# Token-major projections with 512 moving weight columns and one PSUM bank per token tile

## The chip, the core and the metric

The kernel runs on one core of one Trainium2 chip. The metric is the device time of one execution in microseconds. A core has TensorE (PE in the profile, with its weight loads shown as PEld), VectorE (DVE), ScalarE (ACT), GpSimd (POOL) and SyncE (SP), which here issues most DMAs.

## The reference

The reference is a two-layer diffusion backbone over 256 latent tokens and 256 context tokens of width 1024. Each layer normalizes and modulates its input and multiplies it by one combined input projection; three token mixers then work on slices of the result, are merged through gates and an output projection, and are followed by a mixture of experts. Cut to the lines that matter here:

```python
pl = split_cols(h @ w_in)            # latent tokens; pc = the same of the context tokens
qa = apply_rope(rms_norm(to_heads(pl[0], A_HEADS, HEAD_DIM), g_qk[0]), cos, sin)
ka = apply_rope(rms_norm(to_heads(pl[1], A_KV_HEADS, HEAD_DIM), g_qk[1]), cos, sin)
ya, ya_c = gqa_branch(qa, ka, va, qa_c, ka_c, va_c, need_ctx)
qb = rms_norm(to_heads(pl[3], NA_HEADS, HEAD_DIM), g_qk[2])
kb = rms_norm(to_heads(pl[4], NA_HEADS, HEAD_DIM), g_qk[3])
vb = to_heads(pl[5], NA_HEADS, HEAD_DIM)
yb, yb_c = na_branch(qb, kb, vb, qb_c, kb_c, vb_c, rpb, rows, need_ctx)
ym, ym_c = mlstm_branch(...)
y, yc = merge((ya, yb, ym), pl[11], n_tok), ...
x = x + gt1 * y
x = x + gt2 * hier_moe(h, ...)
```

In the second (last) layer the context tokens need no output, so queries are computed for the 256 latent tokens alone, and keys and values for all 512.

## The kernel before

**Tiling.** The normalized input is held feature-major as eight slabs of 128 features by 512 tokens, each split into a high and a low part (`hh`, `hl`) whose sum is the full value. Weights are split in the same way by `wsplit` (lines 207 to 225): ScalarE writes the rounded high part (line 221), VectorE the rest (line 222), in pieces of 128 x 1024 for which there are three buffers each (`whi`, `wlo`). A product is three matmuls into the same PSUM region (`mm3`, lines 332 to 335): high by high, high by low, low by high.

**Token-major and feature-major projections.** `proj_t` (line 490) holds 128 x 128 blocks of the input stationary, one block per token tile of 128 tokens, and moves weight columns: the result has tokens on partitions. One call covers a chunk of 256 weight columns, so that two token tiles share one PSUM bank of 512 columns, and four token tiles take two banks. `proj_f` (line 510) does the opposite: weights stand, 512 tokens (256 in layer 1 where only latent tokens are wanted) move.

**The eight chunks.** After the projections of mixer C (the mLSTM), lines 877 to 901 compute in order: one chunk with the key and value of mixer A (`win[0]`), two chunks of its query, two of the key of mixer B, two of its value and two of its query. Two chunks make one pair of 512 columns. Value chunks are copied to SBUF by VectorE (line 895). Query and key chunks go through `qk_chunk` (line 576), bank by bank: a square on ScalarE (526), a sum over each head on VectorE (528), an addition (532 or 534), a power of -0.5 on GpSimd (536), and a multiplication on VectorE (540), which is the last reader of the bank; latent query tiles of mixer A are then rotated by `do_rope` (VectorE and GpSimd, lines 553 to 558). The transposes back to feature-major (`to_T`, line 561: four 128 x 128 transposes into one bank, lines 570 to 574 evict it on ScalarE) are put into a list `later` and written into the program after the matmuls of the next chunk.

**Fillers.** After its matmuls `proj_t` calls `mod_fill(1)`, which computes one of the adaLN modulation chunks that later stages need: a 1 MB load, 16 matmuls of 32 stationary columns (line 238), an eviction, two transposes (243).

**PSUM.** Of the eight banks four are in the pool `mm`, which serves all projections, the transposes of `to_T` and the modulation chunks; two (`at`), one (`tr`) and one (`ao`) serve the mLSTM scans and the attentions.

**Order of the work.** The scans of the mLSTM stand ahead of the eight chunks in the source, the attention of mixer A behind them. The program is built with `schedule_with_timeline_sim=True` (line 1530): each engine's order of instructions is fixed when the program is built, by a model of the timeline, and parts that stand apart in the source are interleaved. At run time each engine takes its instructions in that order.

Of the kernel before, what the change touches and what calls it, by code (L numbers as in the profile page):

```python
# [24 lines left out]
KT = D // 128  # L25
# [20 lines left out]
def tile_backbone(ctx: ExitStack, tc: tile.TileContext, T, out):  # L46
    nc = tc.nc
# [26 lines left out]
    def t2(shape, dtype=F32, tag="t2", bufs=4):  # L74
        return tp.tile([128] + list(shape), dtype, tag=tag, name=nm(tag), bufs=bufs)
# [4 lines left out]
    def pmm():  # L80
        return bank("mm", 4)
# [53 lines left out]
    ident = cst("ident", [128])  # L135
# [220 lines left out]
    def mixers(l, need_ctx, xsrc, stats):  # L356
# [133 lines left out]
        def proj_t(src, ntt, wid=256):  # L490
# [16 lines left out]
            flush()  # L507
            return banks, views

# [12 lines left out]
        def qknorm(pv, H, is_q):  # L522

            sq = t2([512])
            sqv = sq[:, :2 * H * 64].rearrange("p (t h d) -> p t h d", t=2, d=64)
            nc.scalar.activation(sqv, pv, AF.Square)
            st = small([2 * H])
            nc.vector.tensor_reduce(
                st.rearrange("p (t h) -> p t h", t=2), sqv, axis=AX.X, op=ALU.add)
            v = small([2 * H])  # L530
# [4 lines left out]
            r = small([2 * H])  # L535
            nc.gpsimd.tensor_tensor(out=r, in0=v, in1=powm[:, :2 * H], op=ALU.pow)  # L536
            o = t2([512])
            ov = o[:, :2 * H * 64].rearrange("p (t h d) -> p t h d", t=2, d=64)
            rb = r.rearrange("p (t h) -> p t h", t=2).unsqueeze(3).to_broadcast([128, 2, H, 64])
            nc.vector.tensor_tensor(out=ov, in0=pv, in1=rb, op=ALU.mult)  # L540
            return ov

        def do_rope(x, H, a):
            o = t2([512])
            ov = o[:, :2 * H * 64].rearrange("p (t h d) -> p t h d", t=2, d=64)
            tm = t2([512])
            tv = tm[:, :2 * H * 64].rearrange("p (t h d) -> p t h d", t=2, d=64)

            def tb(j):
                return ropet[:, :, a, j, :].unsqueeze(2).to_broadcast([128, 2, H, 32])  # L550
# [10 lines left out]
        def to_T(parts, H, dst, gain, lat_gain):  # L561

            for p in range(H // 2):
                q = pmm()
                for t in range(2 * len(parts)):
                    src = parts[t // 2][:, t % 2, 2 * p:2 * p + 2, :].rearrange("p h d -> p (h d)")
                    nc.tensor.transpose(q[:, 128 * t:128 * t + 128], src, ident)
                n = 256 * len(parts)
                if lat_gain:
                    nc.scalar.activation(dst(p)[:, :n], q[:, :n], AF.Copy, scale=gain)  # L570
                else:
                    nc.scalar.copy(dst(p)[:, :256], q[:, :256])
                    if n > 256:
                        nc.scalar.activation(dst(p)[:, 256:], q[:, 256:n], AF.Copy, scale=gain)

        def qk_chunk(banks, H, cols, a, is_q, dst, rope_lat):
            parts = []
            for b, bk in enumerate(banks):
                pv = bk.rearrange("p (t c) -> p t c", t=2)[:, :, cols].rearrange("p t (h d) -> p t h d", d=64)
                x = qknorm(pv, H, is_q)  # L580
                if b == 0 and rope_lat:
                    x = do_rope(x, H, a)
                parts.append(x)
            later.append(lambda: to_T(parts, H, dst, gqkT[:, l, a:a + 1], not rope_lat))

        later = []

        def flush():
            while later:
                later.pop(0)()  # L590
# [290 lines left out]
        qk_chunk(banks, 2, slice(0, 128), 1, False, lambda p: kTA, True)  # L881
# [6 lines left out]
        for c in range(2):  # L888
            banks, views = proj_t(win[3 + c], 4)
            qk_chunk(banks, 4, slice(0, 256), 3, False, lambda p, c=c: kTB[:, 2 * c + p], False)  # L890
        vB = s8("qkv", [4, 512])
        for c in range(2):
            banks, views = proj_t(win[5 + c], 4)
            for b in range(2):
                nc.vector.tensor_copy(
                    vB[:, 2 * b:2 * b + 2, 256 * c:256 * c + 256], banks[b].rearrange("p (t c) -> p t c", t=2))
        qTB = s8("qkv", [4, N])
        for c in range(2):
            banks, views = proj_t(win[7 + c], ntq)
            qk_chunk(banks, 4, slice(0, 256), 2, True, lambda p, c=c: qTB[:, 2 * c + p], False)  # L900
        flush()
# [533 lines left out]
def _pack(inputs):  # L1435
    a = {k: np.asarray(v) for k, v in inputs.items()}
    P = 128

    def kmaj(w):
# [30 lines left out]
        w[:, :, cols].reshape(DEPTH, KT, P, 28, 256).transpose(0, 3, 2, 1, 4))  # L1470
    pc = np.concatenate([np.arange(3328, 3328 + 256), np.arange(4352, 4368)])
# [63 lines left out]
```

## Time and profile before

| | |
|---|---|
| median of three runs | 1634.6 us (1631.34 to 1635.05) |
| profiled execution | 1629.37 us |
| its span, first to last instruction | 1627.5 us |
| mean granted TensorE clock | 0.972 of full speed |
| busy: TensorE, VectorE, ScalarE, GpSimd | 1529.6, 788.3, 571.8, 183.2 us |

In a row of a timeline the first number is the start in microseconds from the start of the span, the second the duration; then come engine, source line, operation, what is written and read, partitions x elements, the number of merged instructions and, in brackets, idle time of the engine before it and what ended it. A matmul's duration holds its passage through the array, and successive ones overlap: the spacing of starts tells what one costs in a stream.

### The profile page before, as it was taken

The page shows a single profiled execution, that of the slowest core. Times are in us where ns is not written, and L with a number is a line of the kernel's source. Part 1 is how long each engine was busy: PE and PEld are TensorE (multiplying, and loading weights), DVE is VectorE, ACT ScalarE, POOL GpSimd, SP SyncE. Part 2 cuts the span into 40 slices and gives each one's busy share as a digit, 9 for nine tenths or more (in the row PEclk, how much of TensorE's full clock was granted, in tenths as well). Part 3 has the DMA queues.
Part 4 walks back from the last instruction along what each step waited for, and adds up shares of the span by engine and source line. Part 5 has one row for each costly group of instructions (what it writes and reads, how often), then busy time and mean ns, then how long its engine had stood idle before and what let it go on. Part 6 is the DMA issues. An engine that isn't in the chain of part 4 may idle for free. (4 is left out here: it accounts for less than half of the span.)

```text
span 1627.5 us, 26096 instructions
## 1 busy us (share of the span) xinstructions
PE 1529.6 (94%) x10725; PEld 1058.8 (65%) x10725; DVE 788.3 (48%) x1774; ACT 571.8 (35%) x1125; POOL 183.2 (11%) x162
## 2 busy tenths in 40 slices
PE   5999999999999999989999997999999999897875
PEld 3688789767767778844434435989978789632221
DVE  4637943443345425363333457378456556441222
ACT  4425642443344333131211135356355444211100
POOL 2200320100011003010000003003101112100000
PEclk9999999999999999989999998999999999898888
DMA  8552334323322154349999994542225448699998
GB/s 303 194 172 79 108 107 156 117 76 115 127 98 84 40 179 149 121 166 382 375 398 413 377 409 185 209 142 74 91 104 175 169 148 325 231 411 416 417 418 325
DMA packets 57199, 349.26 MB, mean 215 GB/s; under 512 B 6912, under 2 KB 8032, under 8 KB 20336
## 3 DMA queue, kind: packets, MB, share of 16 engines
q1 hardware_dynamic: 54720, 341.02, 54.9%
q10 hardware_dynamic: 1616, 5.24, 0.9%
q0 software_dynamic: 736, 1.24, 0.4%
q8 instruction: 88, 1.44, 0.4%
q14 instruction: 39, 0.32, 0.1%
HBM read 344.33 MB, written 3.15 MB: 213 GB/s over the span
## 5 line engine op out<-in xcount | busy, mean ns | idle before, releaser
L222 DVE TENSOR_TENSOR wlo<-wraw,whi 128x1024 fp32r<-128x1024 f32 (+1 forms) x152 | 190.6, 1254 | 169.3 <-ACT whi L221 154.2
L333 PE MATMUL mm<-h,whi 128*128 128x512 f32 (+1 forms) x656 | 226.9, 348 | 0.0
L334 PE MATMUL mm<-h,whi 128*128 128x512 f32 (+1 forms) x656 | 223.4, 342 | 0.0
L335 PE MATMUL mm<-h,wlo 128*128 128x512 f32 (+1 forms) x656 | 222.2, 342 | 0.0
L221 ACT CAST whi<-wraw 128x1024 fp32r<-128x1024 f32 (+1 forms) x152 | 155.6, 1026 | 172.3 <-PE mm L334 68.7
L333 PE MATMUL mm<-whi,h 128*128 128x256 f32 (+1 forms) x640 | 183.1, 289 | 0.0
L335 PE MATMUL mm<-whi,h 128*128 128x256 f32 (+1 forms) x640 | 182.9, 288 | 0.0
L334 PE MATMUL mm<-wlo,h 128*128 128x256 f32 (+1 forms) x640 | 182.3, 286 | 0.0
L333 PEld LDWEIGHTS mm<-h,whi 128*128 128x128 f32 x656 | 123.8, 189 | 35.5 <-issue 17.9
L335 PEld LDWEIGHTS mm<-h,wlo 128*128 128x128 f32 x656 | 123.5, 189 | 22.6 <-issue 10.1
L334 PEld LDWEIGHTS mm<-h,whi 128*128 128x128 f32 x656 | 124.2, 190 | 16.9 <-issue 5.3
L333 PEld LDWEIGHTS mm<-whi,h 128*128 128x128 f32 x640 | 121.5, 191 | 6.6 <-issue 4.0
L334 PEld LDWEIGHTS mm<-wlo,h 128*128 128x128 f32 x640 | 122.2, 191 | 1.0 <-DVE G L763 0.5
L335 PEld LDWEIGHTS mm<-whi,h 128*128 128x128 f32 x640 | 121.7, 191 | 1.5 <-issue 1.4
L1274 PE MATMUL at<-qkv,y 128*32 128x512 f32 x792 | 101.2, 606 | 8.0 <-DMA qkv<-in_wgu 8.0
L1208 DVE SCALAR_TENSOR_TENSOR qkv<-mm,c_modT,qkv 128x256 f32<-128x256 f32 x192 | 80.2, 477 | 34.6 <-PE mm L1203 34.6
L618 DVE TENSOR_REDUCE nmx<-at 128x1 f32<-128x512 f32 (+1 forms) x96 | 56.7, 598 | 54.7 <-PE at L604 53.9
L1274 PE MATMUL at<-wraw,y 128*32 128x512 f32 x552 | 73.7, 634 | 7.8 <-DMA wraw<-in_wgu 7.8
L1282 DVE SCALAR_TENSOR_TENSOR a<-a,at 128x256 f32<-128x256 f32 x24 | 10.1, 420 | 141.0 <-ACT a L1281 141.0
L536 POOL TENSOR_TENSOR s1p<-s1p,c_powm 128x8 f32<-128x8 f32 (+1 forms) x24 | 43.3, 1806 | 302.4 <-DVE s1p L534 101.1
L620 ACT ACTIVATE a<-at,nmx 128x512 f32<-128x512 f32 (+1 forms) x96 | 59.3, 619 | 34.3 <-DVE nmx L618 34.1
L1281 ACT ACTIVATE a<-at 128x256 f32<-128x256 f32 x24 | 9.2, 383 | 176.4 <-PE at L1274 171.3
(373 smaller groups left out, 2579.1 us busy)
## 6 DMA issues: line engine op xcount, KB each, us to landing
qkv<-in_wgu SPq DMA_DIRECT2D x62, 1024.0 KB, 11.6
wraw<-in_win SPq DMA_DIRECT2D x56, 1024.0 KB, 4.9
wraw<-in_wgu SPq DMA_DIRECT2D x42, 1024.0 KB, 11.4
wraw<-in_wmod SPq DMA_DIRECT2D x39, 1024.0 KB, 5.0
qkv<-in_wdn SPq DMA_DIRECT2D x31, 1024.0 KB, 9.6
wraw<-in_wdn SPq DMA_DIRECT2D x19, 1024.0 KB, 10.9
h<-in_wgu SPq DMA_DIRECT2D x14, 1024.0 KB, 17.6
wraw<-in_wbr SPq DMA_DIRECT2D x24, 512.0 KB, 3.4
```

The source lines that it names most:

```text
L221: nc.scalar.copy(hv, src)
L222: nc.vector.tensor_sub(lv, src, hv.bitcast(F32))
L333: nc.tensor.matmul(out_, lhsT=lh, rhs=rh, start=first, stop=False)
L334: nc.tensor.matmul(out_, lhsT=lh, rhs=rl, start=False, stop=False)
L335: nc.tensor.matmul(out_, lhsT=ll, rhs=rh, start=False, stop=last)
L536: nc.gpsimd.tensor_tensor(out=r, in0=v, in1=powm[:, :2 * H], op=ALU.pow)
L618: nc.vector.tensor_reduce(nmx[:, hf:hf + 1], S[hf], axis=AX.X, op=ALU.max, negate=True)
L620: nc.scalar.activation(P[hf], S[hf], AF.Exp, bias=nmx[:, hf:hf + 1], scale=1.0, accum_out=sm[:, hf:hf + 1])
L1208: nc.vector.scalar_tensor_tensor(xT[f][:, c], p[:, c], modT[l][:, 40 + f, v_:v_ + 1], xT[f][:, c], op0=ALU.mult, op1=ALU.add)
L1274: nc.tensor.matmul(gps[v_][CAP * e:CAP * e + CAP], lhsT=xe[v_][:, k, s0:s0 + CAP], rhs=w[e], start=(k == 0), stop=(k == KT - 1))
L1281: nc.scalar.activation(th[:, 0:256], gp[:, 0:256], AF.Tanh, bias=0.0, scale=0.5)
L1282: nc.vector.scalar_tensor_tensor(th[:, 0:256], th[:, 0:256], 1.0, gp[:, 0:256], op0=ALU.add, op1=ALU.mult)
```

## The change

The four pairs of chunks (`win[1]` to `win[8]`) become four projections of 512 columns. A new helper `proj_w` takes the weights in two halves of four feature blocks (1 MB each, a new packing `winw`), takes one bank per token tile, and moves 512 weight columns at each stationary block. Within a half it goes through pairs of feature blocks, then token tiles, then the two blocks of the pair. `qk_chunk` now works one token tile of eight heads at a time (four heads of two token tiles before), and `to_T` follows at once: the four transposes of a token tile go into one bank with one eviction. The list `later` is gone. `proj_t` stays for the other chunks. Two modulation chunks follow each projection (`fill2`) instead of one after each chunk.

```diff
+        def proj_w(i, ntt):
+            banks = [pmm() for _ in range(ntt)]
+            for half in range(2):
+                wh, wl = wsplit(wraw(T["winw"][l, i, half], [4, 512]), [4, 512])
+                for kp in range(2):
+                    for t in range(ntt):
+                        c = slice(128 * t, 128 * t + 128)
+                        for j in (2 * kp, 2 * kp + 1):
+                            k = 4 * half + j
+                            mm3(banks[t], hh[k][:, c], hl[k][:, c], wh[j], wl[j], k == 0, k == KT - 1)
+            return banks
...
-        def qknorm(pv, H, is_q):
+        def qknorm(pv, nt_, H, is_q):
+            n = nt_ * H
...
-        def to_T(parts, H, dst, gain, lat_gain):
+        def to_T(x, t0, H, dst, gain):
+            nt_ = x.shape[1]
+            q = pmm()
+            n = 0
             for p in range(H // 2):
-                q = pmm()
-                for t in range(2 * len(parts)):
-                    src = parts[t // 2][:, t % 2, 2 * p:2 * p + 2, :].rearrange("p h d -> p (h d)")
-                    nc.tensor.transpose(q[:, 128 * t:128 * t + 128], src, ident)
...
+                for t in range(nt_):
+                    nc.tensor.transpose(q[:, n:n + 128], x[:, t, 2 * p:2 * p + 2, :].rearrange("p h d -> p (h d)"), ident)
+                    n += 128
...
+        def qk_chunk(pvs, H, a, is_q, dst, rope_lat):
+            t0 = 0
+            for pv in pvs:
+                nt_ = pv.shape[1]
+                roped = t0 < 2 and rope_lat
+                x = qknorm(pv, nt_, H, is_q)
+                if roped:
+                    x = do_rope(x, t0, nt_, H, a)
+                to_T(x, t0, H, dst, None if roped else gqkT[:, l, a:a + 1])
+                t0 += nt_
...
         qTA = s8("qkv", [4, N])
-        for c in range(2):
-            banks, views = proj_t(win[1 + c], ntq)
-            qk_chunk(banks, 4, slice(0, 256), 0, True, lambda p, c=c: qTA[:, 2 * c + p], True)
+        qk_chunk(wide(proj_w(0, ntq)), 8, 0, True, qTA, True)
+        fill2()
...
+        for t, b in enumerate(proj_w(2, 4)):
+            nc.vector.tensor_copy(vB[:, t], b)
+        fill2()
```

The key of mixer B is `proj_w(1, 4)` and its query `proj_w(3, ntq)`, treated as the query of mixer A without rotation; `ntq` is four token tiles in layer 0 and two in layer 1.

## Rows read from the trace of the kernel before

**Rows 1.** Page, parts 1 and 2: busy time; clock and DMA in 40 slices.

```profile
PE 1529.6 (94%) x10725; PEld 1058.8 (65%) x10725; DVE 788.3 (48%) x1774; ACT 571.8 (35%) x1125; POOL 183.2 (11%) x162
...
PEclk9999999999999999989999998999999999898888
DMA  8552334323322154349999994542225448699998
```

**Rows 2.** Table of stretches: us, then busy us (instructions) by engine, clock, DMA.

```profile
162.00:202.00 40.00, 37.31 (x286) 31.35 (x278) 37.50 (x132) 25.66 (x73) 12.36 (x9) 1.00 0.30 106
242.00:282.00 40.00, 40.00 (x347) 36.85 (x347) 13.91 (x26) 11.69 (x19) 1.60 (x1) 1.00 0.44 152
1083.00:1123.00 40.00, 40.00 (x325) 36.14 (x326) 38.18 (x114) 25.94 (x64) 14.42 (x13) 1.00 0.37 120
```

**Rows 3.** Groups by line and shape: narrow matmuls with moving weights, first of three.

```profile
L333 PE MATMUL mm<-whi,h 128*128 128x256 f32 x576 | 165.8, 289 | 0.0
```

**Rows 4.** Timeline of TensorE: first and last of 192 narrow matmuls in a row.

```profile
1159.46 0.39 PE L333 MATMUL mm<-whi,h 128*128 128x256 f32 x1
...
1182.46 0.28 PE L335 MATMUL mm<-whi,h 128*128 128x256 f32 x1
```

**Rows 5.** Timeline of TensorE: first and last of 96 wide matmuls in a row.

```profile
605.82 0.40 PE L333 MATMUL mm<-y,whi 128*128 128x512 f32 x1
...
627.39 0.39 PE L335 MATMUL mm<-y,wlo 128*128 128x512 f32 x1
```

**Rows 6.** Page, parts 5 and 6: a weight split, and the loads of projection weights.

```profile
L222 DVE TENSOR_TENSOR wlo<-wraw,whi 128x1024 fp32r<-128x1024 f32 (+1 forms) x152 | 190.6, 1254 | 169.3 <-ACT whi L221 154.2
...
wraw<-in_win SPq DMA_DIRECT2D x56, 1024.0 KB, 4.9
```

**Rows 7.** Instructions of line 895, the value's copies: min/median/max ns.

```profile
L895 DVE COPY qkv<-mm x8: 690/690/692, 248.0 to 1171.3; 128x512 f32<-128x512 f32 x8
```

**Rows 8.** Instructions of lines 567 and 570: transposes and evictions, min/median/max ns.

```profile
L567 PE MATMUL mm<-c_ident,t x88: 272/273/330, 162.6 to 1188.2; 128*128 128x128 f32 x88
...
L570 ACT ACTIVATE qkv<-mm,c_gqkT x16: 472/682/714, 233.6 to 1189.3; 128x512 f32<-128x512 f32 x12, 128x256 f32<-128x256 f32 x4
```

**Rows 9.** Timeline, layer 0, query of A: chunks' ends and starts, last bank readers.

```profile
161.43 0.28 PE L335 MATMUL mm<-whi,h 128*128 128x256 f32 x1
...
168.24 0.47 PE L333 MATMUL mm<-whi,h 128*128 128x256 f32 x1
...
172.48 0.69 DVE L540 TENSOR_TENSOR t<-mm,s1p 128x512 f32<-128x512 f32 x1 [0.52 <-POOL s1p L536]
...
183.36 0.67 DVE L540 TENSOR_TENSOR t<-mm,s1p 128x512 f32<-128x512 f32 x1
...
197.65 0.68 DVE L540 TENSOR_TENSOR t<-mm,s1p 128x512 f32<-128x512 f32 x1
...
207.63 0.69 DVE L540 TENSOR_TENSOR t<-mm,s1p 128x512 f32<-128x512 f32 x1 [0.48 <-POOL s1p L536]
```

**Rows 10.** Table of a stretch, line 333 alone: TensorE's and its loads' busy us (instructions).

```profile
162.00:202.00 40.00, 14.75 (x52) 9.87 (x52) 1.00 0.30 106
```

**Rows 11.** Timeline, layer 1, second key chunk of B: its two banks' way.

```profile
1142.09 0.60 ACT L526 ACTIVATE t<-mm 128x512 f32<-128x512 f32 x1 [0.24 <-PE mm L335]
...
1142.48 0.28 PE L335 MATMUL mm<-whi,h 128*128 128x256 f32 x1
1142.72 0.69 DVE L528 TENSOR_REDUCE s1p<-t 128x8 f32<-128x512 f32 x1 [2.90 <-ACT t L526]
...
1143.69 1.64 POOL L536 TENSOR_TENSOR s1p<-s1p,c_powm 128x8 f32<-128x8 f32 x1 [5.46 <-DVE s1p L534]
...
1145.04 0.36 PE L333 MATMUL mm<-whi,h 128*128 128x256 f32 x1
...
1146.22 0.68 DVE L540 TENSOR_TENSOR t<-mm,s1p 128x512 f32<-128x512 f32 x1
...
1149.45 0.69 DVE L540 TENSOR_TENSOR t<-mm,s1p 128x512 f32<-128x512 f32 x1 [0.66 <-POOL s1p L536]
```

More of the change, by code (lines that the diff above doesn't have):

```diff
@@ L534, in qknorm, with do_rope @@
                 nc.vector.tensor_scalar(v, st, 1.0 / 64, EPS, op0=ALU.mult, op1=ALU.add)
-            r = small([2 * H])
-            nc.gpsimd.tensor_tensor(out=r, in0=v, in1=powm[:, :2 * H], op=ALU.pow)
+            r = small([n])
+            nc.gpsimd.tensor_tensor(out=r, in0=v, in1=powm[:, :n], op=ALU.pow)
             o = t2([512])
-            ov = o[:, :2 * H * 64].rearrange("p (t h d) -> p t h d", t=2, d=64)
-            rb = r.rearrange("p (t h) -> p t h", t=2).unsqueeze(3).to_broadcast([128, 2, H, 64])
+            ov = o[:, :64 * n].rearrange("p (t h d) -> p t h d", t=nt_, d=64)
+            rb = r.rearrange("p (t h) -> p t h", t=nt_).unsqueeze(3).to_broadcast([128, nt_, H, 64])
             nc.vector.tensor_tensor(out=ov, in0=pv, in1=rb, op=ALU.mult)
             return ov
-        def do_rope(x, H, a):
+        def do_rope(x, t0, nt_, H, a):
             o = t2([512])
-            ov = o[:, :2 * H * 64].rearrange("p (t h d) -> p t h d", t=2, d=64)
+            ov = o[:, :64 * nt_ * H].rearrange("p (t h d) -> p t h d", t=nt_, d=64)
             tm = t2([512])
-            tv = tm[:, :2 * H * 64].rearrange("p (t h d) -> p t h d", t=2, d=64)
+            tv = tm[:, :64 * nt_ * H].rearrange("p (t h d) -> p t h d", t=nt_, d=64)
             def tb(j):
-                return ropet[:, :, a, j, :].unsqueeze(2).to_broadcast([128, 2, H, 32])
+                return ropet[:, t0:t0 + nt_, a, j, :].unsqueeze(2).to_broadcast([128, nt_, H, 32])
             x1, x2 = x[:, :, :, 0:32], x[:, :, :, 32:64]
@@ L576, in qk_chunk @@
[L576 to L586, printed above, removed]
@@ L588, in flush @@
-        def flush():
-            while later:
-                later.pop(0)()
+                for t in range(nt_):
+                    nc.tensor.transpose(q[:, n:n + 128], x[:, t, 2 * p:2 * p + 2, :].rearrange("p h d -> p (h d)"), ident)
+                    n += 128
+            v = q[:, :n].rearrange("p (h t) -> p h t", h=H // 2)
+            d = dst[:, :, 128 * t0:128 * (t0 + nt_)]
+            if gain is None:
+                nc.scalar.copy(d, v)
+            else:
+                nc.scalar.activation(d, v, AF.Copy, scale=gain)
@@ new lines, in qk_chunk, with fill2, wide @@
+        def qk_chunk(pvs, H, a, is_q, dst, rope_lat):
[8 more added lines that the diff above has]
+                t0 += nt_
+        def fill2():
+            mod_fill(2, stop=16 + 2 if l == 0 else 0)
+        def wide(banks):
+            return [b.rearrange("p (t h d) -> p t h d", t=1, d=64) for b in banks]
@@ L880, in mixers @@
                 vA[:, 2 * b:2 * b + 2], banks[b].rearrange("p (t c) -> p t c", t=2)[:, :, 128:256])
-        qk_chunk(banks, 2, slice(0, 128), 1, False, lambda p: kTA, True)
+        qk_chunk([b.rearrange("p (t c) -> p t c", t=2)[:, :, 0:128].rearrange("p t (h d) -> p t h d", d=64) for b in banks],
+                 2, 1, False, kTA.unsqueeze(1), True)
         qTA = s8("qkv", [4, N])
-        for c in range(2):
-            banks, views = proj_t(win[1 + c], ntq)
-            qk_chunk(banks, 4, slice(0, 256), 0, True, lambda p, c=c: qTA[:, 2 * c + p], True)
+        qk_chunk(wide(proj_w(0, ntq)), 8, 0, True, qTA, True)
+        fill2()
         kTB = s8("qkv", [4, N])
-        for c in range(2):
-            banks, views = proj_t(win[3 + c], 4)
-            qk_chunk(banks, 4, slice(0, 256), 3, False, lambda p, c=c: kTB[:, 2 * c + p], False)
+        qk_chunk(wide(proj_w(1, 4)), 8, 3, False, kTB, False)
+        fill2()
         vB = s8("qkv", [4, 512])
[L892 to L896, printed above, removed]
+        for t, b in enumerate(proj_w(2, 4)):
+            nc.vector.tensor_copy(vB[:, t], b)
+        fill2()
         qTB = s8("qkv", [4, N])
[L898 to L901, printed above, removed]
+        qk_chunk(wide(proj_w(3, ntq)), 8, 2, True, qTB, False)
+        fill2()
         yhA, ylA = s8pair("qkv", nq)
@@ L1470, in _pack @@
         w[:, :, cols].reshape(DEPTH, KT, P, 28, 256).transpose(0, 3, 2, 1, 4))
+    T["winw"] = np.ascontiguousarray(
+        w[:, :, cols[256:256 * 9]].reshape(DEPTH, 2, 4, P, 4, 512).transpose(0, 4, 1, 3, 2, 5))
     pc = np.concatenate([np.arange(3328, 3328 + 256), np.arange(4352, 4368)])
```

16 lines of the change are left out of this document (4 added, 12 removed).

## The prediction

> **What bounds the kernel now.** The page comes first. TensorE is busy for 1529.6 us, 94% of the span, VectorE for less than half of it, and the clock line stands at full speed in nearly all of the first 17 slices and again in slices 26 to 34; DMA is at nine tenths or more only in slices 19 to 24 and 36 to 39, the two mixtures of experts [rows 1]. The projections that change lie in the token mixers, far from the DMA-bound ends. So I next read a table of stretches there [rows 2]. The reader is to see two kinds of stretch. In 242 to 282 us, layer 0, TensorE has no idle time while VectorE works 14 of 40 us. In 162 to 202 us, where the mLSTM scans run between the projections, TensorE idles 2.7 us (40.00 less 37.31) and VectorE is busy 37.5 us. In layer 1 the corresponding stretch, 1083 to 1123 us, has VectorE busy 38.2 us but no idle TensorE. So TensorE's instruction stream sets the time nearly everywhere; in two stretches VectorE is close to taking over. A microsecond of matmul stream saved here arrives at the end, since the later stages follow in order and start earlier by as much, the experts' loads with them (they go into buffers that the mixers release).
>
> **What the wide matmuls save.** The groups by shape count 576 narrow matmuls of 256 columns in the first of the three lines of the split product [rows 3]. The eight chunks have 8 x 8 x 4 = 256 of them in layer 0 and 192 in layer 1 (two token tiles instead of four for the queries), 448 together; the other 128 are the chunks that stay narrow. Three lines make 1344 narrow matmuls, which become 672 wide ones of 512 columns. A matmul's duration says nothing on its cost in a stream, so I take spacings: 192 narrow ones start between 1159.46 and 1182.46 us, 23.00 / 191 = 120.4 ns each [rows 4]; 96 wide ones start between 605.82 and 627.39 us, 21.57 / 95 = 227.1 ns each [rows 5]. Both streams swap a 128 x 128 stationary block at each matmul, as the new one will. The 256 added columns cost 106.7 ns, which is 256 columns at 2.4 GHz; 13.8 ns is left as the price of an instruction. The stream loses 1344 x 120.4 - 672 x 227.1 = 161.8 - 152.6 = 9.2 us. That is the whole direct gain, since the multiplications are the same. Its lower end is 0, if a wide one cost two narrow ones.
>
> The Trainium skill, page "TensorE: Matmul & The Clock Gate", section "Back-to-back issue gap", gives the isolated warm spacing as the columns over 2.4 GHz plus 2.5 ns. By that estimate two narrow ones take 218.4 ns, a wide one 215.8 ns, and the 672 pairs save only 1.7 us. The rows disagree: each spacing lies above the rule's, by 11.2 and 11.3 ns, so the fixed part here is 13.8 ns.
>
> **What comes at no price.** Weight loads remain 1 MB each and as many; one lands in 4.9 us [rows 6], while half a layer-0 projection, 48 wide matmuls, occupies TensorE for 10.9 us, so they stay hidden behind it. On SP's queue the two weight halves now stand ahead of two modulation loads instead of alternating with them; if that cover were gone, a projection's start would wait up to 4.9 us once. The splits keep their number and size, 1.25 us on VectorE per piece [rows 6]; a piece served 48 narrow matmuls (5.8 us) and serves 24 wide ones (5.4 us). The normalizing operations keep count and shape (eight heads of one tile instead of four heads of two), and so do the rotations, the 88 transposes and VectorE's eight copies of the value [rows 7, 8]. ScalarE has a few evictions fewer, off the path at 35% busy. Sixteen matmuls per modulation chunk move, none is added. TensorE's transposes now come right behind the chain of their tile instead of a chunk later: if the fixed order puts them too early, the next projection's matmuls queue behind them; that wait is part of what follows.
>
> **What it adds: waits for banks.** A pair of banks served a chunk while the pool's other two served the next. Now a four-tile projection takes all four, and the next one, the transposes and the modulation chunks get one only when a tile's chain has ended with its multiplication on line 540. I bound this at each hand-over.
>
> Query of A to key of B, layer 0. Now the first query chunk's last matmul starts at 161.43 us; the four query banks have their last reader's end at 173.17, 184.03, 198.33 and 208.32 us, and the second chunk starts at 168.24 us [rows 9]. The pace is (208.32 - 161.43) / 4 = 11.7 us per bank, because VectorE is full. These waits cost TensorE little: two chunk boundaries lie in 162 to 202 us, and it idles 2.7 us [rows 2], since the scans feed it (line 333 has 52 matmuls here [rows 10], so 156 narrow ones, 18.8 us, and 18.5 us of other work in 40, 46%). After the change one boundary is left, of four banks, and the transposes free their inputs sooner. Ends: -2.7 us (that idle time goes) and +12.6 us (worked out under the rivals). I take 0, the row as it stands: one boundary twice as dear as each of the two now.
>
> Query to key in layer 1: the query has only two tiles, so two banks are free; VectorE is as full, TensorE idles nothing now [rows 2]. Ends 0 and 6.3 us, taken 0.
>
> Key to value of B, both layers. Here VectorE has room. The chain of one bank goes from the square at 1142.09 to the multiplication's end at 1146.90 us, 4.8 us; the second bank follows at 1150.14, 3.2 us later [rows 11]. Now the next chunk starts at 1145.04 us in the other pair, before either is free; this cover goes. In the new order tile 0 is complete 3 x 6 matmuls = 4.1 us ahead of the last tile, so its bank comes free 0.7 us after the end, and then one every 3.2 us. If TensorE ran just the six matmuls that source order gives each tile (1.36 us), it would idle 0.7 + 3 x (3.2 - 1.36) = 6.2 us. Against this stand 16 transposes, the modulation chunks and, above all, the attention of mixer A, which needs nothing from the pool `mm`; a tile can also run ahead through the weight pieces that lie ready. Ends 0 and 6.2 us per layer; I take 1.5 each, 3.0 together, nearer to the full stretch of 242 to 282 us, where nothing idles.
>
> Value to query of B: the value's banks are released by copies of 0.69 us [rows 7] while its tiles end 1.36 us apart, so nothing.
>
> **Sum.** -9.2 + 0 + 0 + 3.0 = -6.2 us. The profiled execution took 1629.37 us, 1.9 us more than its span, and would go to 1623.2 us. It lies 5.2 us below the median of the runs shown; on the median, 1634.6 us, the forecast is 1628.4 us. A measurement of this kernel can tell about 0.3%, 4.9 us, from no change, so the gain is just above that.
>
> **Rivals.**
>
> *The bank hand-over costs more than the stream saves.* Place: query of A to key of B in the two stretches where VectorE is full. If the key cannot begin before two of the query's four banks are free, it waits 23.4 us at the pace of 11.7, and other work covers 46%: 12.6 us idle. Layer 1 waits for one bank more than now, half of that, 6.3 us. -9.2 + 18.9 = +9.7 us, 1644.3 us. For it: every bank of the pool is taken when the query's matmuls end, and VectorE serves the scans, which stand first in the source, ahead of the chain. Against it: twice as many boundaries cost 2.7 us now, and a tile does not need the other tiles' banks. It decides for slower when the waits pass 14.1 us. Chance 0.22.
>
> *The waits eat the gain.* Waits of 4.3 to 14.1 us, say 9 us by three of the four hand-overs at half their upper end: 1634.4 us. Chance 0.24.
>
> *A wide matmul costs two narrow ones.* The fixed 13.8 ns would belong to the stationary block with its columns and not to the instruction, the stream would keep its length, and the 3.0 us of waits would stand alone: 1637.6 us. Against it speak 96 matmuls in a row at 227.1 ns [rows 5]. Chance 0.04. The skill's rule named above comes close to this case.
>
> *The forecast* and what lies beyond it on its side (the 2.7 us of idle time go as well: 1625.7 us; without the 3.0 us of waits too, 1622.7 us): chance 0.50.
>
> **How the numbers follow.** Faster by over 0.3%: 0.50, of which nearly all lies between 1622 and 1629.7 us. Within 0.3%: 0.24 + 0.04 = 0.28. Slower: 0.22, about half of it above 1644 us. The range reaches from 1621 us, just under the best sum (1622.7 us), to 1644 us, the price of the slower rival; that leaves out somewhat more than one in ten above and less than one below. The forecast's own range is 1622 to 1632 us.
>
> **What would show it.** Wide matmuls `mm<-whi,h` spaced at 227 to 230 ns show the saving; 240 ns would make the first step wrong. Right behind the query of A in layer 0 (about 180 to 200 us) the table of stretches should show no more than some 3 us of idle TensorE, and behind the keys about 1 or 2 us; idle time ended by line 540 or by an eviction of line 570's kind, of more than 10 us in all, would make the forecast wrong and the first rival right. If the wide spacing holds, the hand-overs idle little, and the time still does not fall, then something outside this stage has moved: the order of the scans or attentions, or the start of the experts' loads, and my claim that a saved microsecond arrives at the end is what failed.

## The result, and the profile after

The changed kernel takes 1655.87 us (median of four runs, 1648.59 to 1660.34) against 1632.97 us (four runs) before: a ratio of 1.0138, 95% interval 1.0092 to 1.0183. It is slower by about 22.5 us; 6 us of gain had been forecast, and the time lies above the predicted range. The profiled execution took 1660.34 us, 31 us more than the one of before.

The page of the kernel after, span, busy time of the engines and granted clock by slice, answers to [rows 1]:

```profile
span 1658.1 us, 24765 instructions
...
PE 1539.8 (93%) x10053; PEld 1034.0 (62%) x10053; DVE 784.8 (47%) x1774; ACT 573.7 (35%) x1117; POOL 173.2 (10%) x162
...
PEclk9999997999999999979999998999999999899898
```

Two things have changed. Span less busy time was 1627.5 - 1529.6 = 97.9 us and is 118.3 us: TensorE idles 20.4 us more. And it is busy 10.2 us longer although its stream has become cheaper; the clock line shows a 7 in its seventh slice (249 to 290 us), where it was a 9. The first loss is a wait, the second a clock.

**The stream became cheaper, as forecast.** The groups by shape, line 333 of after, answer to [rows 3]: the 576 narrow matmuls are 224 wide and 128 narrow ones.

```profile
L333 PE MATMUL mm<-whi,h 128*128 128x512 f32 x224 | 87.3, 398 | 0.0
...
L333 PE MATMUL mm<-whi,h 128*128 128x256 f32 x128 | 37.2, 290 | 0.0
```

The timeline of TensorE after, layer 1, first and last of 96 wide matmuls in a row, answers to [rows 4, 5]:

```profile
1189.34 0.48 PE L333 MATMUL mm<-whi,h 128*128 128x512 f32 x1
...
1210.97 0.39 PE L335 MATMUL mm<-whi,h 128*128 128x512 f32 x1
```

They stand (1210.97 - 1189.34) / 95 = 227.7 ns apart; 227.1 had been taken.

**The hand-overs became long.** This table of stretches of after answers to [rows 2]; its columns are the same. Each row runs from the last matmul of one projection to the first of the next: query of A to key of B and key to value of B in layer 0, then the same two in layer 1.

```profile
181.80:214.90 33.10, 25.99 (x172) 19.75 (x170) 27.75 (x86) 22.32 (x69) 13.30 (x11) 0.90 0.03 9
237.70:267.40 29.70, 27.18 (x134) 14.01 (x132) 15.50 (x38) 15.24 (x35) 6.55 (x4) 0.66 0.11 36
1132.90:1150.50 17.60, 11.62 (x82) 7.83 (x80) 13.70 (x27) 8.71 (x24) 10.60 (x10) 0.90 0.18 70
1172.90:1189.30 16.40, 15.16 (x88) 8.28 (x87) 13.54 (x28) 11.55 (x26) 5.99 (x3) 1.00 0.07 29
```

Before, no two chunks of the eight lay more than 10.0 us apart in layer 0 (184.2 to 194.2 us), or 5.0 in layer 1. A long stretch alone costs nothing, as TensorE does scan and attention work in it that must be done anyway. What it costs stands in two columns: idle time, 7.1 + 2.5 + 6.0 + 1.2 = 16.9 us in the four (from the unrounded columns), and the clock, 0.66 in the second.

A hand-over that the forecast doesn't name grew as well: from the narrow chunk with the key and value of A to the query of A, in layer 0 and in layer 1.

```profile
138.30:151.70 13.40, 12.46 (x82) 8.31 (x81) 11.91 (x44) 6.77 (x17) 3.09 (x4) 1.00 0.38 142
1098.10:1117.60 19.50, 16.51 (x100) 11.56 (x99) 18.34 (x65) 12.46 (x33) 4.49 (x5) 0.91 0.20 68
```

Before, it took 4.0 and 4.9 us (138.30 to 142.31 and 1078.57 to 1083.46). It idles 0.9 and 3.0 us now, the latter at a clock of 0.91. This chunk is as narrow as before and holds two banks; only its transposes are placed otherwise.

What fills the longest, query of A to key of B in layer 0, is seen on the timeline of TensorE of after (in brackets, idle time before the row and what ended it); it answers to [rows 9]:

```profile
181.53 0.40 PE L335 MATMUL mm<-whi,h 128*128 128x512 f32 x1
...
186.78 0.66 PE L96 MATMUL tr<-c_ident,mg 128*128 128x128 f32 x4 [2.42 <-ACT a L99]
...
193.49 0.60 PE L582 MATMUL mm<-c_ident,t 128*128 128x128 f32 x4
...
200.76 0.60 PE L582 MATMUL mm<-c_ident,t 128*128 128x128 f32 x4
...
203.68 0.63 PE L96 MATMUL tr<-c_ident,y 128*128 128x128 f32 x4 [2.32 <-DVE y L846]
...
207.71 0.93 PE L582 MATMUL mm<-c_ident,t 128*128 128x128 f32 x4
...
212.49 0.60 PE L582 MATMUL mm<-c_ident,t 128*128 128x128 f32 x4
213.02 1.93 PE L238 MATMUL mm<-wraw,c_cpad 128*32 128x256 f32 x32
214.89 0.50 PE L333 MATMUL mm<-whi,h 128*128 128x512 f32 x1
```

And on VectorE of after: line 554 is the multiplication that frees a bank (line 540 before), line 222 the second part of the next projection's weights.

```profile
183.80 0.68 DVE L554 TENSOR_TENSOR t<-mm,s1p 128x512 f32<-128x512 f32 x1
184.40 1.21 DVE L222 TENSOR_TENSOR wlo<-wraw,whi 128x1024 fp32r<-128x1024 f32 x1
...
195.83 0.69 DVE L554 TENSOR_TENSOR t<-mm,s1p 128x512 f32<-128x512 f32 x1
...
205.08 0.69 DVE L554 TENSOR_TENSOR t<-mm,s1p 128x512 f32<-128x512 f32 x1
...
209.59 0.69 DVE L554 TENSOR_TENSOR t<-mm,s1p 128x512 f32<-128x512 f32 x1 [1.75 <-POOL s1p L550]
```

The reader is to see two things. The first is the order: all four groups of the query's transposes (line 582) and both modulation chunks (line 238) come ahead of the next projection's first matmul at 214.89 us, and each group can't come before its tile's chain through ScalarE, VectorE and GpSimd. The second is the bank. Weights lie ready from 185.6 us and a first bank is free from 184.5, but the next projection doesn't get it. The bank of every tile is fixed when the program is built (the built program has these matmuls in the order of the trace). There the transposes and the two modulation chunks take the banks of the query's first three tiles, and the key's first bank is that of its last tile, free at 210.28 us (209.59 + 0.69). TensorE idles 2.42 us up to 186.78 and 2.32 us up to 203.68, each time for work of the scans. So of the 33 us, 28.7 pass before the key has a bank (181.53 to 210.28) and 4.6 after that, behind transposes and modulation chunks. Before, the second query chunk began at 168.24 us, 4.9 us ahead of the end of the first chunk's first multiplication [rows 9].

The Trainium skill, page "PSUM — Partial Sum Buffer", section "Engine vs sequencer instructions", says that matmuls start and complete in program order. The trace agrees in those last 4.6 us: the key's first bank is free at 210.28 us, and its first matmul waits behind the transposes at 212.49 and the modulation chunks at 213.02.

**The clock.** Table of stretches of after inside the second hand-over; next-to-last but one is the granted clock.

```profile
238.00:244.00 6.00, 4.63 (x33) 2.55 (x31) 3.79 (x7) 4.22 (x8) 3.27 (x2) 1.00 0.51 175
244.00:248.00 4.00, 2.85 (x13) 1.96 (x14) 3.30 (x9) 2.80 (x8) 0.17 (x1) 0.74 0.00 0
248.00:252.00 4.00, 4.00 (x14) 1.84 (x16) 1.97 (x6) 2.08 (x8) 1.47 (x1) 0.50 0.00 2
252.00:264.00 12.00, 12.00 (x42) 5.83 (x39) 4.76 (x13) 4.41 (x10) 1.64 (x1) 0.50 0.00 1
264.00:267.40 3.40, 3.40 (x37) 1.55 (x35) 1.51 (x4) 1.73 (x4) 0.00 (x0) 0.65 0.02 5
```

From 248 to 264 us the clock is 0.50, the 1.2 GHz level, and TensorE is fully busy: only transposes and attention matmuls are left, all at half speed. It had idled 1.15 of the 4 us before. So here busy time, too, is a loss.

**Where the 31 us stand.** The mixers of both layers, from the first scan to the last attention matmul in layer 0 and to the last score matmul of the last attention in layer 1, table of stretches, before:

```profile
122.20:604.80 482.60, 479.91 (x3034) 367.06 (x3031) 243.08 (x569) 205.38 (x442) 56.98 (x42) 1.00 0.31 105
1062.50:1309.50 247.00, 245.95 (x1866) 207.57 (x1864) 159.25 (x326) 126.36 (x257) 44.56 (x32) 1.00 0.36 124
```

and after, with the two parts of layer 0 that have a lower clock:

```profile
122.20:620.50 498.30, 486.18 (x2648) 354.71 (x2646) 241.69 (x569) 206.28 (x438) 54.53 (x42) 0.97 0.29 102
1082.00:1335.80 253.80, 242.91 (x1546) 190.17 (x1543) 154.88 (x324) 126.28 (x253) 39.35 (x31) 0.99 0.34 117
...
120.00:200.00 80.00, 75.59 (x473) 59.95 (x472) 66.07 (x236) 47.49 (x120) 12.20 (x12) 0.98 0.21 75
200.00:300.00 100.00, 93.83 (x504) 67.50 (x504) 39.81 (x89) 35.74 (x81) 13.59 (x9) 0.88 0.30 108
```

Layer 0 takes 15.7 us more. Idle time grows from 2.7 to 12.1, 9.4 us; the clock takes 80 x 0.02 + 100 x 0.12 = 13.6 us; the cheaper stream gives 384 x (2 x 120.4 - 227.1) ns = 5.3 us. That sums to 17.7 us, 2 too many: idle time at the low clock is counted twice, and the clock is read to two places. Layer 1 takes 6.8 us more: idle time grows by 9.8 us, the clock of 0.99 takes some 2.5, the stream gives 3.9; that is 8.4 us, 1.6 too many (32 matmuls of modulation chunks have also left this stretch). Of the 8.1 us left of the span's difference, 3.8 lie between the mixers of the two layers (457.7 us before, 461.5 after) and 3.9 between the end of the second stretch and layer 1's router, where those 32 matmuls stand now; the cause of the 3.8 was not followed. This execution is also 4.5 us above the median.

### The profile page after: what moved, and what is told of

Same layout as the page of the kernel before. It is cut to its first block, busy times and chain, and to the rows that moved or that the text cites. A ratio compares the mean times of both kernels' runs of the same rounds, so it can differ in the third digit from the quotient of the medians.

```text
span 1658.1 us, 24765 instructions
## 1 busy us (share of the span) xinstructions
PE 1539.8 (93%) x10053; PEld 1034.0 (62%) x10053; DVE 784.8 (47%) x1774; ACT 573.7 (35%) x1117; POOL 173.2 (10%) x162
## 5 line engine op out<-in xcount | busy, mean ns | idle before, releaser
L335 PE MATMUL mm<-whi,h 128*128 128x512 f32 (+2 forms) x416 | 143.4, 347 | 0.0
L334 PE MATMUL mm<-wlo,h 128*128 128x512 f32 (+2 forms) x416 | 143.4, 346 | 0.0
L333 PE MATMUL mm<-whi,h 128*128 128x512 f32 (+2 forms) x416 | 141.8, 348 | 0.0
L333 PEld LDWEIGHTS mm<-whi,h 128*128 128x128 f32 x416 | 78.1, 189 | 14.1 <-issue 4.7
L334 PEld LDWEIGHTS mm<-wlo,h 128*128 128x128 f32 x416 | 78.6, 189 | 9.3 <-issue 0.7
L335 PEld LDWEIGHTS mm<-whi,h 128*128 128x128 f32 x416 | 78.6, 189 | 9.3 <-issue 1.0
L1294 DVE SCALAR_TENSOR_TENSOR a<-a,at 128x256 f32<-128x256 f32 x24 | 10.1, 421 | 140.9 <-ACT a L1293 140.9
```

Of the source, the lines that this page charges most:

```text
L333: nc.tensor.matmul(out_, lhsT=lh, rhs=rh, start=first, stop=False)
L334: nc.tensor.matmul(out_, lhsT=lh, rhs=rl, start=False, stop=False)
L335: nc.tensor.matmul(out_, lhsT=ll, rhs=rh, start=False, stop=last)
L1294: nc.vector.scalar_tensor_tensor(th[:, 0:256], th[:, 0:256], 1.0, gp[:, 0:256], op0=ALU.add, op1=ALU.mult)
```

## The experiments

Theories. **Order**: the transposes stand directly behind their chain in the program, so TensorE's next projection stands behind chain and transposes. **Banks**: a projection holds all four banks of the pool until its multiplications have ended. The two are not independent: a transpose written earlier also gets a bank of the pool earlier. Each run has its ratio to the kernel before with its 95% interval; `later` is the list that put transposes behind the next chunk's matmuls.

**Copy first.** The changed kernel, with each bank copied to SBUF by ScalarE, and the chain working on the copy.

```diff
+                for t, pv in enumerate(pvs):
+                    c = dst[:, :, 128 * t:128 * t + 128]
+                    nc.scalar.copy(c, pv.rearrange("p t h d -> p (t h d)").rearrange("p (a b) -> p a b", b=128))
+                    held.append(c.rearrange("p a (e d) -> p a e d", d=64))
+                for t, x in enumerate(held):
+                    x = qknorm_sb(x, is_q)
```

> The changed kernel, but each of the four banks of a query or key projection is copied to SBUF by ScalarE first (into the slab region that its transposes fill later), and the whole chain of squares, powers, multiplication and rotation works on that copy, so that a bank is held for one copy of about 0.6 us instead of the chain. Bank theory (the next projection waits because one projection holds all four banks of the pool until its tiles' chains end): the gaps without projection matmuls in layer 0, 33 us behind the query of A and 30 us behind the key of B, shrink to the time of transposes and modulation chunks, under 15 us each, and the time falls to 1622 to 1640 us. Order theory (the transposes placed at once and two modulation chunks in a row stall TensorE, whoever holds the banks): the gaps stay and the time is 1648 us or more.

Measured: 1643.89 us, ratio 1.0083 (1.0060 to 1.0106), between what either theory expected. The hand-over from query of A to key of B still lasts 31.8 us (180.9 to 212.7), key to value of B falls from 29.9 to 11.9. Banks have a part, and it isn't all. In the program as built, the query's transposes take all four banks that the copies have freed, and the key's first bank is that of the third group of transposes.

**Narrow chunks in the new order.** The kernel before, transposes at once and two modulation chunks behind each pair.

```diff
-            later.append(lambda: to_T(parts, H, dst, gqkT[:, l, a:a + 1], not rope_lat))
+            to_T(parts, H, dst, gqkT[:, l, a:a + 1], not rope_lat)
...
+        fill2()
```

> The kernel before with its narrow chunks in two banks, but in the changed kernel's source order: transposes right behind each chunk's chain instead of a chunk later, and two modulation chunks after each pair instead of one after each chunk. Bank theory: two banks stay free for the next chunk, so little is lost, 1629 to 1640 us. Order theory: the order alone costs most of the 23 us, 1648 to 1660 us.

Measured: 1657.12 us, 1.0151 (1.0129 to 1.0174). A chunk holds only two banks here, no matmul is wide, and a loss of the same size is there. Why this costs some 8 us less than the same order with single modulation chunks (three runs further on) was not settled.

**Hold four banks.** The kernel before; each chunk of four heads and four token tiles takes the pool's other two banks as well and gives them back after its last multiplication.

```diff
+            hold = hold_two() if H == 4 and len(banks) == 2 else []
...
+                if b == len(banks) - 1:
+                    let_go(hold, x)
```

> The kernel before, with narrow chunks and its old order, but each chunk of a query or key in four heads also takes the other two banks of the pool: one transpose of the identity is written into each, and eight columns of each are read only after the chunk's last multiplication (two small VectorE additions and two transposes more per chunk, ten chunks of four tiles or fewer, together under 6 us of work). Bank theory: no chunk can start before the chain of the one before has ended, in more places than in the changed kernel, so 1650 to 1690 us. Order theory and any other that does not rest on the banks: at most 6 us more than before, 1633 to 1640 us.

Measured: 1642.22 us, 1.0063 (1.0040 to 1.0085). Some 10 us in the old order, less than the banks theory needs, more than the order theory allowed. By the estimate above up to 6 us of it may be the edit's own work, so the held banks themselves cost some 4 to 10 us here.

**Two tiles at a time.** The changed kernel with two passes per projection of two tiles and two banks each, weights loaded and split again for the second.

```diff
+            for g in range(ntt // 2):
+                banks = [pmm() for _ in range(2)]
```

> The changed kernel with wide matmuls, but queries and keys are projected for two token tiles at a time, so that two banks are held as before; the weights are loaded and split again for the second pair of tiles (24 pieces more, 1.03 us on ScalarE and 1.26 us on VectorE each). Bank theory: the next pair of tiles runs while the chains of the pair before hold their banks; most of the loss goes, 1628 to 1645 us, the rest being VectorE's extra splits where it is full. Order theory: transposes at once remain, 1648 us or more.

Measured: 1659.63 us, 1.0169 (1.0147 to 1.0190); the longest hand-over is 33.8 us. Holding two banks in place of four doesn't help as long as transposes are written at once; the added splits on VectorE blur this comparison.

**Transposes at once, alone.** The kernel before with that one edit, and modulation chunks as they were.

```diff
-            later.append(lambda: to_T(parts, H, dst, gqkT[:, l, a:a + 1], not rope_lat))
+            to_T(parts, H, dst, gqkT[:, l, a:a + 1], not rope_lat)
```

> The kernel before, narrow, and only the transposes written right behind each chunk's chain; modulation chunks stay where they were. Theory of source order of the transposes: this one edit costs what the new order costs, 1648 to 1660 us, with gaps of over 10 us without projection matmuls behind the query chunks of mixer A. Rival (modulation chunks in a row): 1628 to 1640 us.

Measured: 1664.36 us, 1.0200 (1.0183 to 1.0217). One edit costs 33 us. In the program as built, the transposes wait in the two banks that are free, and the next chunk gets the very banks of the chunk before, when its chain ends. The run that holds four banks likewise gives the next chunk banks of the chunk before, but with late transposes, and costs 10 us; so far as these two runs go, the larger part of the 33 us comes with the transposes ahead of the chunk.

**Modulation chunks in pairs, alone.** The kernel before.

```diff
-            banks, views = proj_t(win[1 + c], ntq)
+            banks, views = proj_t(win[1 + c], ntq, fill=2 * c)
```

> The kernel before, narrow, with late transposes, and only the modulation chunks moved: two behind the second chunk of each pair in place of one behind each. Theory of source order of the transposes: little changes, 1628 to 1638 us. Rival (the modulation chunks in a row, each with a bank of the pool and 16 matmuls, are what the new order costs): 1645 us or more.

Measured: 1633.10 us, 1.0022 (1.0012 to 1.0032): 3.6 us. Here one stretch between chunks also lasts 18.2 us (175.2 to 193.4), idles 3.0 us and has its clock at 1.00, which shows again that a stretch's length is not its price.

**Transposes in another bank.** The changed kernel, the transposes in the one bank that serves the transposes of scans and attentions.

```diff
-            q = pmm()
+            q = ptr()
```

> The changed kernel with its immediate transposes written into the pool tr (one bank, shared with scans and attentions) instead of the pool mm, one word. If the loss comes from the grant of mm banks in source order, the next projection no longer stands behind the transposes but only behind the chain that frees its banks and the modulation chunks: part of the loss goes, 1635 to 1649 us. If it is TensorE's own order of instructions that puts the transposes first, whatever their bank: unchanged, 1650 to 1662 us, or slower by the sharing.

Measured: 1693.62 us, 1.0385 (1.0356 to 1.0413). That is far above what was expected, and worse than the pool of four: query of A to key of B takes 63.5 us in the table of stretches, TensorE idles 19.9 of them at a mean clock of 0.72 (its table of stretches, then two rows of its timeline).

```profile
171.60:235.10 63.50, 43.56 (x218) 28.73 (x216) 40.58 (x135) 28.56 (x84) 14.39 (x12) 0.72 0.17 55
```

```profile
140.32 0.50 PE L333 MATMUL mm<-whi,h 128*128 128x512 f32 x1
...
219.57 0.69 PE L582 MATMUL tr<-c_ident,t 128*128 128x128 f32 x2 [0.78 <-ACT mg L875]
```

The two rows tell more than the time. The query of A begins at 140.32 us, 4.0 us behind the chunk with A's key and value (13.5 in the changed kernel), and that chunk's transposes, written ahead of it in the source, follow at 219.57 us. So being written earlier doesn't by itself put transposes ahead of a projection; here, where they take no bank of its pool, they stand behind. The query's own first three groups come ahead of the key again; in the program as built, the key's first bank is that of the query's third tile.

**Next chunk's banks first.** Is it the order, or that the transposes take the free banks? The kernel before with transposes at once, but the next chunk's two banks are asked for ahead of theirs.

```diff
+            if nxt:
+                early.append([pmm() for _ in range(nxt)])
+            to_T(parts, H, dst, gqkT[:, l, a:a + 1], not rope_lat)
```

> The kernel before (narrow chunks) with the transposes written directly behind each chain, as in the run that had this edit alone (ratio 1.020, hand-overs of 8 to 20 us), but the next chunk's two banks are taken from the pool ahead of the banks of these transposes. Theory G (what costs is the grant: the transposes take the pool's free banks first, and the next chunk must then wait for a bank of the chain itself): the next chunk has free banks again, its matmuls need not wait, hand-overs fall to 3 to 10 us, ratio 0.998 to 1.008. Theory O (the fixed order of TensorE places transposes that stand earlier in the source ahead of the next chunk's matmuls whatever the banks, so that the chunk stands behind chain and transposes): hand-overs stay at 8 to 20 us, ratio 1.014 to 1.024. In between (1.008 to 1.014): both have a part.

Measured: 1664.66 us, 1.0205 (1.0180 to 1.0230): no different from at once alone. But the edit changed nothing: the 10725 matmuls of both traces follow each other in the same order, and in the program as built each has the same bank in both. The next chunk's banks are still those of the chunk before, and the transposes wait in the two free ones. So this run repeats that one and doesn't part order from banks. The timeline of TensorE, first query chunk of A to the second, layer 0 (line 570 is the transpose), and the first chunk's first multiplication on VectorE:

```profile
177.15 0.28 PE L335 MATMUL mm<-whi,h 128*128 128x256 f32 x1
...
196.13 0.60 PE L570 MATMUL mm<-c_ident,t 128*128 128x128 f32 x4
196.48 0.36 PE L333 MATMUL mm<-whi,h 128*128 128x256 f32 x1
```

```profile
189.76 0.68 DVE L543 TENSOR_TENSOR t<-mm,s1p 128x512 f32<-128x512 f32 x1
```

The second chunk comes 19.3 us behind the end of the first, where before it came 6.8 us behind (161.43 to 168.24). Its first bank is free after 13.3 us, at 190.44; another 6.0 us pass behind the first four transposes, which wait for the rotation too. Order and banks both have a part.

**Wide, transposes late.** The changed kernel with the list `later` put back; the tiles that now wait longer got six buffers in place of four.

```diff
-    def t2(shape, dtype=F32, tag="t2", bufs=4):
+    def t2(shape, dtype=F32, tag="t2", bufs=6):
...
-                to_T(x, t0, H, dst, None if roped else gqkT[:, l, a:a + 1])
+                later.append(lambda x=x, t0=t0, roped=roped: to_T(x, t0, H, dst, None if roped else gqkT[:, l, a:a + 1]))
```

> The changed kernel (wide projections, four banks, the chain ends each bank's use) with one thing put back: the transposes of a projection are written behind the matmuls of the next one, as before the change. No copy of the banks. Theory O (the place of the transposes is the whole loss, the four banks cost nothing much): the stream's 9 us arrive, ratio 0.992 to 0.998. Theory B (a projection that holds all four banks until its multiplications have ended costs as much as in the run in which four banks were held in narrow chunks, +10.7 us, less the 9 us of the stream): ratio 0.998 to 1.006, with hand-overs of 10 us and more behind the query of A and the key of B in layer 0. If it is 1.010 or more, late transposes don't help without the copies, and the copies were what made the combined version faster.

Measured: 1640.88 us, 1.0062 (1.0044 to 1.0080), just past the top end of what the banks theory expected, with its long hand-overs (35.0 and, from key to value, 11.0 us); the order alone is excluded as the whole cause. Its table of stretches and then TensorE's timeline, query of A to key of B:

```profile
172.90:207.60 34.70, 27.30 (x153) 17.44 (x151) 34.41 (x119) 20.25 (x62) 12.99 (x10) 0.80 0.28 99
```

```profile
172.64 0.39 PE L335 MATMUL mm<-whi,h 128*128 128x512 f32 x1
...
186.39 1.94 PE L238 MATMUL mm<-wraw,c_cpad 128*32 128x256 f32 x16 [1.52 <-ACT kva L589]
...
197.02 1.94 PE L238 MATMUL mm<-wraw,c_cpad 128*32 128x256 f32 x16
...
207.61 0.50 PE L333 MATMUL mm<-whi,h 128*128 128x512 f32 x1 [0.73 <-DVE t L554]
```

VectorE of the same kernel, the first three multiplications:

```profile
182.79 0.69 DVE L554 TENSOR_TENSOR t<-mm,s1p 128x512 f32<-128x512 f32 x1
...
195.00 0.68 DVE L554 TENSOR_TENSOR t<-mm,s1p 128x512 f32<-128x512 f32 x1
...
206.88 0.68 DVE L554 TENSOR_TENSOR t<-mm,s1p 128x512 f32<-128x512 f32 x1
```

Now the wait names the bank: the projection starts 0.05 us after the third multiplication's end, 207.56 us. The two modulation chunks come behind the first and the second one; no row names their banks, but in the program as built they have those of the query's first two tiles, and the key begins in the third's. TensorE idles 7.4 us in this stretch, and its clock is 0.80.

**Copy first, and transposes late.** Both remedies, with rotation in place and the modulation chunks ahead of the chain.

```diff
+                    nc.scalar.copy(c, pv.rearrange("p t h d -> p (t h d)").rearrange("p (a b) -> p a b", b=128))
...
+                fill2()
+                flush()
...
+                    later.append(lambda x=x, t=t, roped=roped: to_T_sb(x, t, dst, None if roped else gqkT[:, l, a:a + 1]))
```

> Wide matmuls with the banks copied to SBUF first (as in the run with the copy) and, in addition, the transposes of a projection written a projection later again, behind the next one's matmuls and copies (the rotation writes in place so that nothing waits in a buffer of VectorE's). Theory of source order (banks of the pool are granted in source order, so transposes written at once put the whole chain of a projection in front of the next projection's first matmul): the gaps without projection matmuls fall under 8 us each, the 9 us of the wide stream show, 1618 to 1632 us. Rival (the four banks, or the wide matmuls in themselves, keep TensorE waiting): still 1640 us or more.

Measured: 1623.17 us against 1630.24, ratio 0.9962 (0.9947 to 0.9976), faster than both kernels. Its page, and its three hand-overs in layer 0 (query to key, key to value, value to query):

```profile
span 1618.2 us, 24753 instructions
...
PE 1525.4 (94%) x10053; PEld 1024.1 (63%) x10053; DVE 785.3 (49%) x1774; ACT 583.1 (36%) x1137; POOL 180.0 (11%) x162
```

```profile
171.20:177.70 6.50, 6.50 (x60) 4.15 (x59) 5.64 (x21) 4.75 (x13) 1.02 (x2) 1.00 0.93 311
208.80:218.00 9.20, 8.60 (x79) 5.92 (x79) 8.05 (x25) 6.40 (x16) 2.02 (x2) 1.00 0.81 311
243.50:250.00 6.50, 6.50 (x69) 4.98 (x69) 2.56 (x8) 5.02 (x15) 0.00 (x0) 1.00 0.40 135
```

The hand-overs are short, 0.6 us is idle, and the clock is full. Span less busy time is 92.8 us.

**The two remedies together.** Four kernels have the same wide stream. In us against before, each ratio less one times the 1630 to 1633 us of its own runs of before:

| | transposes late | transposes at once |
|---|---|---|
| banks copied first | -6.2 | +13.5 |
| banks held by the chain | +10.1 | +22.5 |

Late transposes are worth 12.4 us with held banks and 19.7 with copied ones; copies are worth 9.0 us with transposes at once and 16.3 with late ones. The changed kernel's interval, 15 to 30 us, leaves the 12.4 and the 9.0 uncertain by some 8 us, and the other two are uncertain by some 4. The rows and columns are edits and not pure causes: both act on who has a bank of the pool when. The upper left kernel also has the rotation in place and the modulation chunks ahead of the chain. How much of its gain is theirs no run shows: the chunks in pairs alone cost 3.6 us, and in the lower left kernel they take two banks ahead of the key. That kernel also has the six buffers.

## Why the prediction was wrong, point by point

**The stream: right.** 227.7 ns instead of 227.1, and with both remedies a gain arrives: -6.2 us. That this is also the forecast's sum is chance, as that kernel has copies and another order that the forecast didn't price. That a microsecond saved here arrives at the end held in the other direction: of layer 0's loss of 15.7 us nothing was won back later. The isolated warm spacing that the Trainium skill gives (page "TensorE: Matmul & The Clock Gate", section "Back-to-back issue gap"), 215.8 ns and 1.7 us by it, is not the spacing of this stream.

**"What comes at no price", the transposes: this is the step that failed.** It named the danger, that the next projection's matmuls queue behind transposes put too early, and then called that wait part of the hand-overs, where no term was worked out for it; there the transposes even counted in favour ("the transposes free their inputs sooner"). Measured, this edit costs 33 us alone in narrow chunks, and 12.4 us with wide ones whose banks are held as in the change. The list `later` was read as a detail of the code; it is what gives the next chunk a place and a bank ahead of transposes that wait for a chain through three other engines. How the 33 us divide between place and bank no run shows exactly.

**Query of A to key of B, 0 us: failed.** It idles 7.1 us at a clock of 0.90. The argument that more than half of TensorE's time there is fed by the projections and the rest by scans took the other work to be at hand whenever the projection waits; it ran out twice, for 2.4 and 2.3 us, and the wait grew to 33 us. Query to key in layer 1, also 0, idles 6.0 us. The hand-over from A's key and value to its query, 3.9 us idle in both layers, had no term at all.

**Key to value, 1.5 us each: fair as idle time, but not the whole price.** 2.5 and 1.2 us idle, and the first also has its clock at 0.66 over 29.7 us, 10.1 us of lost speed. No term of the sum had the clock in it, and [rows 2] had it at 1.00 throughout.

**The rival of dear hand-overs.** Its price, +9.7 us, is close to the +10.1 of held banks with late transposes, and its place is right: there the key began when the third bank came free, where it had supposed the second. That the sum agrees is partly luck: in layer 0 it had 12.6 us idle, where 7.4 are idle and a clock of 0.80 over 34.7 us, which it didn't count, takes 6.9. In layer 1 it was wrong by some 5 us: 6.3 expected, and only 1.3 us idle there when transposes are late. It lacked the 12.4 us of the transposes at once, so that even this rival fell short of 22.5. The mark set beforehand, more than 10 us of idle time at the hand-overs, was passed with 16.9, but it looked for idle time ended by line 540: in the changed kernel that doesn't show, because the key's first matmul, when its bank has come free, still stands behind something else.

**The other terms at no price.** The modulation chunks, whose move had been put at nothing, cost 3.6 us in pairs alone, in narrow chunks. Loads, splits and copies of the value weren't tried alone, but the fastest kernel has them all as the change has them, and it is 6.2 us faster than before.

## What to carry to other kernels

When a change removes a list that puts work off, price that first: ask what will stand behind the moved instruction on its engine, whose bank it will take, and how long the chain is that it waits for. Before a run is taken as proof, see that its edit changed the program: asking for banks earlier did not. The table of stretches between two blocks of the main stream shows the damage in two columns, idle time and clock; a long stretch with neither is free. When one block takes all of a pool's banks and a long chain reads them last, copying them out first and writing the transposes a block later helped together; neither remedy alone was enough here.

## What the hardware showed that was not expected

TensorE's clock fell to its 1.2 GHz level for 16 us in which the engine was busy throughout (248 to 264 us, 0.50), after 4 us with 1.15 us idle at 0.74. Attention matmuls and transposes alone ran there; it was back at the next projection's first matmuls (0.23 us apart from 267.72 us). So this late projection cost twice, once by idle time and once by the speed of what ran instead. The Trainium skill, page "TensorE: Matmul & The Clock Gate", section "A second HAM failure mode: psum-queue depth-cycling", tells of a kernel whose groups of matmuls cycle through PSUM banks with small idle times between them and whose clock swings between the two levels. In this trace, too, small idle times stand ahead of the fall (4.63 of 6 and 2.85 of 4 us busy), but it is one fall and no swinging. With the short hand-overs of the fastest kernel the clock is 1.00 in all three stretches shown.
